# A transformer layer on one core: the first norm over four loads with a pivot, and first groups of one feature tile

## The chip, the cores and the metric

The kernel runs on one core of a Trainium2 chip. The metric is device microseconds (us) of one execution. A core has a matrix engine (TensorE, in the profile PE, with its weight loads as PEld), three engines for element-wise work (VectorE or DVE, ScalarE or ACT, GpSimd or POOL), and queues that issue DMA transfers, of which SyncE's (SP) brings nearly all data here. Each engine runs its own instructions strictly in the order in which they were written down, and waits on semaphores for what others make.

## The reference

One layer over 288 tokens (256 of a prompt, 8 sequences of 4), width 2048, all in float32, cut to what the change touches:

```python
mod = jax.nn.silu(c) @ w_ada + b_ada                      # 9 rows of c, 6 * 2048 columns
sh1, sc1, g1, sh2, sc2, g2 = jnp.split(mod[:, None, :], 6, axis=-1)
h = layer_norm(x) * (1 + sc1) + sh1
z = (h @ w_in).astype(f32)                                # 7176 columns
# ... two kinds of recurrent heads over z, output projection, two norms,
#     a gated convolutional FFN of width 5504, a last norm
```

`layer_norm` takes off the mean over the 2048 features and divides by the root of the variance plus 1e-5.

## The kernel before, in words

Features lie on partitions, tokens along the free axis: x is 16 tiles `xs[k]` of [128, 288]. TensorE multiplies weights as two exact parts, high and low, so a k-tile of 128 features times a column of 128 outputs takes three matmuls of 288 columns: high weights times the high and the low part of h, low weights times the high part. Weights stream in **granules** of up to 1024 columns (512 KB each): SP loads `raw`, ScalarE casts the high part (`whi`), VectorE subtracts to get the low part (`wlo`).

`start()` does the following, and the order in which it is written is the order on each engine.
- It loads x, then forms the mean: `colsum` adds up the features by a product with ones, `total` adds the four partial sums. It subtracts the mean from each tile, squares, adds up again, and takes `rx`, the inverse root, with one Newton step.
- The adaLN projection runs in **steps** (`ada_step`), each on 512 KB of `w_ada` (`araw`, four buffers, so a load waits until the step four before it has run). Steps form **units**: the shifts and scales of a few feature tiles. When the last step of a unit is done, `ada_finish` transposes its sums and writes `mod`, and `hidden(k)` makes h of each of its tiles on VectorE (times `rx`, times scale plus shift), with a cast on ScalarE (`split`) and a subtraction for the low part.
- The first 28 output columns of w_in are multiplied **group** by group: a group is some k-tiles (`KG`), for which its granules go through all 28 columns. The products of a column in a group stand in a PSUM bank until `partial` takes them into `z`: by a copy on ScalarE in the first group, by an add on VectorE in later ones. Banks alternate between tags `mm` (two buffers) and `sd` (five, shared with adaLN units and sums). Between granules some adaLN steps run, by a fixed rule.
- A group can begin when all its tiles of h exist.

Before, `KG` is (2, 2, 4, 4, 4), so the first two groups have 7 granules of 4 columns, 0.8 us of products a column, and units hold (2, 2, 2, 2, 4, 4) tiles. Eight steps run before the first product. `mixer()` follows with the last group, the other columns, the heads and the output projection, `tail()` with the rest. x lies in 16 buffers of the pool of [128, 288] tiles that everything shares.

Lines of the profile: L168 is every matmul, L155 tensor-tensor, L158 scalar-tensor-tensor, L162 tensor-scalar, L165 activation, L188 the cast of `split`, L228 the cast of weights, L389 the copy in `total`, L339 the transpose of a unit, L497 the copy of a column, L307 and L219 the loads of `w_ada` and weights, L436 of x.

Of the kernel before, what the change touches and what calls it, by code (L numbers as in the profile page):

```python
# [17 lines left out]
P = 128  # L18
# [30 lines left out]
KG = (2, 2, 4, 4, 4)  # L49
ADA_K = (2, 2, 2, 2, 4, 4)  # L50
# [74 lines left out]
def _ada_units():  # L125
    """The adaLN projection in units of 4 or 8 feature tiles (of 6 * 16)"""
    u, k = [], 0
    for n in ADA_K:
        u.append([16 * m + k + q for m in range(2) for q in range(n)])
        k += n  # L130
    return u + [[16 * m + 8 * z + q for q in range(8)] for m in range(2, 6) for z in range(2)]
# [6 lines left out]
class K:  # L138
    """One pass over the layer: features on partitions, the 288 tokens along the free axis.

    The weights stream through in granules of 1024 columns, each split into two exact parts of 12 bits;
    between granules the recurrences of the finished heads advance by a few steps.
    """
# [9 lines left out]
    # ---------------------------------------------------------------- small helpers  # L153
# [30 lines left out]
    def split(self, src, hi=None, lo=None):  # L184
        """src = hi + lo exactly, both of 12 significant bits."""
# [6 lines left out]
    # ---------------------------------------------------------------- weight stream  # L192
    def queue_weights(self):
        i, q = self.i, []
        for g, ks in enumerate(KG):
            if g == len(KG) - 1:
                q.append(i["w_gate"])
            q += [i[f"w_in_a{g}"][p] for p in range(NSPLIT * ks // GK)]
# [48 lines left out]
    def products(self, ps, hl, c0, xs, first, last, w=P):  # L247
        """ps += (hi + lo) of the weight tiles at columns c0... times xs, in three exact passes."""
# [15 lines left out]
    # ---------------------------------------------------------------- interleaving  # L264
    def tick(self):
        """advance the background work"""
# [4 lines left out]
    def slot(self):  # L271
        """Between two granules: advance the recurrences and the adaLN stream."""
# [10 lines left out]
    def later(self, *fs):  # L283
        """one of fs in each of the next slots"""
# [6 lines left out]
    def settle(self):  # L291
        """emit what is still to come of the background work"""
        while self.bg:
            self.tick()

    # ---------------------------------------------------------------- adaLN parameters
# [13 lines left out]
    def ada_step(self):  # L310
        """A k-tile or two of the columns of a unit of silu(c) @ w_ada, a quarter of the columns per column tile
        of the array: column tile q has the features 32 q ... 32 q + 31 of each of the unit's feature tiles."""
# [50 lines left out]
    # ---------------------------------------------------------------- statistics  # L363
    def rstd_of(self, v, pool=False):
        """v ** -0.5 with one Newton step; [128, 288]."""
# [15 lines left out]
    def colsum(self, ps, t, k, n):  # L381
        """partial sums over the features, in four column tiles of the array"""
# [3 lines left out]
    def total(self, ps):  # L386
        """32 times the sum of the partial sums, on every partition"""
# [6 lines left out]
    def log1pexp(self, src):  # L394
        """ln(1 + exp(-|src|))"""
# [6 lines left out]
    # ---------------------------------------------------------------- program  # L402
    def run(self):
# [21 lines left out]
        self.start()  # L425
# [3 lines left out]
    def start(self):  # L429
        """LN of x; then, as the adaLN parameters of each four k-tiles arrive, those k-tiles of h."""  # L430
# [3 lines left out]
        xs = self.xs = [self.t288() for _ in range(KT)]  # L434
        for k in range(KT):
            nc.sync.dma_start(xs[k], i["xt"][:, k, :])  # L436
        self.ada_load(NA)
        a, b = CC["cap"][0], PK["b_ada"][1]
        nc.sync.dma_start(self.cs[:, :a], i["cst"][:, :a])
        nc.sync.dma_start(self.pks[:, :b], i["pk"][:, :b])  # L440
# [8 lines left out]
        sm = self.ps(T)  # L449
        for k in range(KT):  # L450
# [1154 lines left out]
```

## Time and profile before

| | us |
|---|---|
| three runs | 1624.29, 1624.74, 1627.13 (median 1624.74) |
| profiled execution, span from first to last instruction | 1626.7 |
| TensorE busy | 1575.5 (97%) |
| VectorE busy | 1033.7 (64%) |
| ScalarE busy | 696.8 (43%) |
| GpSimd busy | 295.0 (18%) |
| chain that ended last | TensorE 87%, VectorE 8%, ScalarE 2%, DMA 1% |

The profiled execution has no other time than its span; this lies 2.0 us above the median of the runs. Busy times overlap, so they don't add up to the span. The chain that ended last is followed back from the last instruction, at each step to what released it; its shares say where the time is decided.

### The profile page before, as it was taken

What the parts mean: (1) busy time and instruction counts of PE and PEld (TensorE: products, weight loads), DVE (VectorE), ACT (ScalarE), POOL (GpSimd) and SP (SyncE); (2) the same over time, 40 slices, a digit from 0 to 9 for tenths busy, and PEclk for the clock granted to TensorE, in tenths of its full rate; (3) what the DMA queues carried; (4) which work ended last, traced back from release to release, by engine and by line L of the source; (5) the groups of instructions that cost most, each with busy time, mean ns of one, the idle gap of its engine ahead of it and who ended that gap; (6) DMA issues with size and microseconds to landing.
All of it is one profiled execution on the core that took longest, in us unless ns stands there. A gap on an engine that the chain in (4) does not pass through costs nothing.

```text
span 1626.7 us, 31719 instructions
## 1 busy us (share of the span) xinstructions
PE 1575.5 (97%) x12577; PEld 1445.1 (89%) x12577; DVE 1033.7 (64%) x2068; ACT 696.8 (43%) x1222; POOL 295.0 (18%) x450
## 2 busy tenths in 40 slices
PE   6999999999999999998999999999999999999995
PEld 3988889788888878886999999999999999999984
DVE  4566667877778778778865554455555455555445
ACT  3423235564655655435643433344443334334332
POOL 1000011444343343214411100011110001111012
PEclk9999999999999999999999999999999999999997
DMA  8988855767868777882545555555455554555441
GB/s 283 342 329 307 303 193 177 267 233 271 284 229 314 240 282 269 305 328 101 167 167 169 166 162 162 172 167 166 163 163 159 168 172 166 169 168 157 150 133 59
DMA packets 99268, 340.78 MB, mean 209 GB/s; under 512 B 11433, under 2 KB 18097, under 8 KB 98097
## 3 DMA queue, kind: packets, MB, share of 16 engines
q1 hardware_dynamic: 96624, 328.55, 59.8%
q0 software_dynamic: 2496, 10.22, 1.6%
q8 instruction: 99, 1.62, 0.4%
q14 instruction: 49, 0.39, 0.1%
HBM read 326.51 MB, written 12.21 MB: 208 GB/s over the span
## 4 chain that ended last, share of the span: by engine, by line
PE 87%; DVE 8%; ACT 2%; DMA 1%; issue 1%; SPq 0%; POOL 0%; ACTq 0%; DVEq 0%
PE mm L168 70%; PE sd L168 13%; PE ad L168 4%; DVE t L155 4%; DVE wlo L155 1%; DVE t L158 1%; ACT t L165 1%; DVE c L158 1%; ACT whi L228 1%; DVE t L162 1%; DMA araw<-w_ada 0%; DMA t<-xt 0%; DMA raw<-w_up_a 0%; PE sd L697 0%; PE sd L1066 0%
## 5 line engine op out<-in xcount | busy, mean ns | idle before, releaser
L168 PE MATMUL mm<-t,whi 128*128 128x288 f32 (+1 forms) x4624 | 940.4, 298 | 14.6 <-ACT whi L228 9.2
L168 PEld LDWEIGHTS mm<-t,whi 128*128 128x128 f32 (+1 forms) x4624 | 740.7, 188 | 39.2 <-issue 19.3
L168 PE MATMUL mm<-t,wlo 128*128 128x288 f32 x2312 | 682.6, 295 | 1.1 <-DVE wlo L155 1.1
L228 ACT CAST whi<-raw 128x1024 fp32r<-128x1024 f32 (+2 forms) x413 | 422.8, 1026 | 476.0 <-PE mm L168 242.2
L155 DVE TENSOR_TENSOR wlo<-raw,whi 128x1024 fp32r<-128x1024 f32 (+2 forms) x413 | 502.5, 1218 | 21.3 <-ACT whi L228 8.7
L168 PEld LDWEIGHTS mm<-t,wlo 128*128 128x128 f32 x2312 | 435.6, 188 | 1.7 <-DVE wlo L155 1.7
L168 PE MATMUL mm<-ff,whi 128*128 128x288 f32 x1376 | 276.8, 297 | 0.0
L168 PEld LDWEIGHTS mm<-ff,whi 128*128 128x128 f32 x1376 | 220.4, 188 | 6.2 <-issue 5.1
L168 PE MATMUL mm<-ff,wlo 128*128 128x288 f32 x688 | 203.1, 295 | 0.0
L165 ACT ACTIVATE t<-t 128x288 f32<-128x288 f32 (+4 forms) x328 | 125.7, 396 | 176.3 <-DVE t L155 117.6
L155 POOL TENSOR_TENSOR t<-t,t 128x288 f32<-128x288 f32 (+3 forms) x159 | 142.0, 903 | 294.6 <-ACT t L165 102.8
L158 DVE SCALAR_TENSOR_TENSOR t<-mm,mod,t 128x256 f32<-128x256 f32 x96 | 46.3, 483 | 155.7 <-PE mm L168 149.6
L168 PEld LDWEIGHTS mm<-ff,wlo 128*128 128x128 f32 x688 | 129.1, 188 | 0.0
L155 DVE TENSOR_TENSOR t<-t,t 128x288 f32<-128x288 f32 (+5 forms) x219 | 106.9, 508 | 34.1 <-ACT t L188 27.2
L1404 POOL COPY convo<-ext 128x2 f32<-128x2 f32 x43 | 7.9, 184 | 630.6 <-ACT ext L1398 630.6
L1399 DVE COPY ext<-mm 128x32 f32<-128x32 f32 x42 | 8.1, 192 | 141.9 <-ACT ext L1398 141.9
L168 PE MATMUL sd<-t,whi 128*128 128x288 f32 x464 | 95.9, 299 | 0.0
L168 PE MATMUL ad<-araw,csp 128*32 128x256 f32 (+1 forms) x1312 | 90.1, 368 | 5.8 <-DVE adsb L339 4.0
L168 PEld LDWEIGHTS sd<-t,whi 128*128 128x128 f32 x464 | 76.0, 192 | 0.0
L155 DVE TENSOR_TENSOR t<-t,mm 128x288 f32<-128x288 f32 x70 | 31.5, 451 | 65.5 <-PE mm L168 65.2
L155 DVE TENSOR_TENSOR t<-cv,mm 128x256 f32<-128x256 f32 x80 | 20.8, 301 | 78.3 <-PE mm L168 78.3
L168 PE MATMUL sd<-t,wlo 128*128 128x288 f32 x232 | 69.2, 298 | 0.0
(233 smaller groups left out, 1160.0 us busy)
## 6 DMA issues: line engine op xcount, KB each, us to landing
araw<-w_ada SPq DMA_DIRECT2D x180, 512.0 KB, 5.2
raw<-w_up_b SPq DMA_DIRECT2D x160, 512.0 KB, 3.6
raw<-w_in_a SPq DMA_DIRECT2D x56, 512.0 KB, 6.1
raw<-w_in_b SPq DMA_DIRECT2D x56, 512.0 KB, 5.3
raw<-w_down SPq DMA_DIRECT2D x48, 512.0 KB, 3.5
raw<-w_down SPq DMA_DIRECT2D x32, 384.0 KB, 3.1
raw<-w_out_a SPq DMA_DIRECT2D x16, 512.0 KB, 5.8
raw<-w_out_b SPq DMA_DIRECT2D x16, 512.0 KB, 6.0
```

The lines of the kernel that those rows point to most:

```text
L155: (eng or self.nc.vector).tensor_tensor(out=out, in0=a, in1=b, op=op)
L158: self.nc.vector.scalar_tensor_tensor(out=out, in0=a, scalar=s, in1=b, op0=op0, op1=op1)
L162: (eng or self.nc.vector).tensor_scalar(out=out, in0=a, scalar1=s1, scalar2=s2, op0=op0, **kw)
L165: self.nc.scalar.activation(out, a, f, **kw)
L168: self.nc.tensor.matmul(out, lhsT, rhs, start=start, stop=stop, **kw)
L228: self.nc.scalar.copy(hi[:, :w], raw[:, :w])
L1399: nc.vector.tensor_copy(se[:, :, 2:6], self.smp(pa))
L1404: nc.gpsimd.tensor_copy(co[:, j, 0:2], ext[:, TP:TP + 2])
```

## The change: what it does

x comes in four loads of four tiles into one tile `x` of a pool of its own (`xin`), which is closed after `start()`. The mean of the first four tiles is a **pivot**; it is taken off every tile as it lands (VectorE three of four, GpSimd one of four), ScalarE squares what is left, and two sums run side by side, of the deviations (`s1`) and of their squares (`s2`). The variance is the mean square less the square of the mean deviation `d`. `d` itself is taken off later: on GpSimd for tiles 4 to 15, and in `hidden` on VectorE for the first four.

`KG` becomes (1, 1, 2, 4, 4, 4), with granules of 7 columns of one tile, 4 columns of two tiles and 2 columns of four (`PER`); units hold (1, 1, 2, 4, 4, 4) tiles. Four steps run before the first product, and `ADA_DUE` says how many steps go into each group, spread over all its granules but the last. There is one granule more (57 for 56), and 28 more adds into `z`.

```diff
-KG = (2, 2, 4, 4, 4)
-ADA_K = (2, 2, 2, 2, 4, 4)
+KG = (1, 1, 2, 4, 4, 4)
+ADA_K = (1, 1, 2, 4, 4, 4)
+ADA_DUE = (4, 10, 16, 16, 24)
+PER = {1: 7, 2: 4, 4: 2}
...
-        xs = self.xs = [self.t288() for _ in range(KT)]
-        for k in range(KT):
-            nc.sync.dma_start(xs[k], i["xt"][:, k, :])
+        xt = xin.tile([P, KT, T], F32, name="x")
+        for k in range(0, KT, 4):
+            nc.sync.dma_start(xt[:, k:k + 4, :], i["xt"][:, k:k + 4, :])
+        xs = self.xs = [xt[:, k, :] for k in range(KT)]
         self.ada_load(NA)
         a, b = CC["cap"][0], PK["b_ada"][1]
+        nc.sync.dma_start(self.pks[:, :b], i["pk"][:, :b])
+        self.load_to(2)
         nc.sync.dma_start(self.cs[:, :a], i["cst"][:, :a])
-        nc.sync.dma_start(self.pks[:, :b], i["pk"][:, :b])
...
-        sm = self.ps(T)
-        for k in range(KT):
-            self.colsum(sm, xs[k], k, KT)
-        mu = self.t288()
-        self.tsc(mu, self.total(sm), 1.0 / (32 * D), None, ALU.mult)
-        self.ada_step()
-        self.ada_step()
-        sq = self.ps(T)
-        for k in range(KT):
-            self.tt(xs[k], xs[k], mu, ALU.subtract, eng=nc.gpsimd if k % 3 == 2 else None)
-            s = self.t288()
-            if k % 4 == 3:
-                self.tt(s, xs[k], xs[k], ALU.mult)
-            else:
+        pv = self.ps(T)
+        for k in range(4):
+            self.colsum(pv, xs[k], k, 4)
+        piv = self.t288()
+        nc.scalar.mul(piv, self.total(pv), 1.0 / (32 * 4 * P))
+        s1, s2 = self.ps(T), self.ps(T)
+        for c in range(0, KT, 4):
+            sq = []
+            for k in range(c, c + 4):
+                self.tt(xs[k], xs[k], piv, ALU.subtract, eng=nc.gpsimd if k % 4 == 2 else None)
+                s = self.t288()
                 self.act(s, xs[k], AF.Square)
-            self.colsum(sq, s, k, KT)
-            if k % 4 == 1:
-                self.ada_step()
-        var = self.t288()
-        self.tsc(var, self.total(sq), 1.0 / (32 * D), EPS, ALU.mult, ALU.add)
+                sq.append(s)
+            for k in range(c, c + 4):
+                self.colsum(s1, xs[k], k, KT)
+            for k in range(c, c + 4):
+                self.colsum(s2, sq[k - c], k, KT)
+        t1, t2 = self.total(s1), self.total(s2)
+        var, w = self.t288(), self.t288()
+        d = self.d = self.t288()
+        self.act(var, t2, AF.Identity, scale=1.0 / (32 * D), bias=self.eps)
+        self.tsc(d, t1, 1.0 / (32 * D), None, ALU.mult)
+        self.tt(w, d, d, ALU.mult)
+        self.tt(var, var, w, ALU.subtract)
         self.rx = self.rstd_of(var)
+        for k in range(4, KT):
+            self.tt(xs[k], xs[k], d, ALU.subtract, eng=nc.gpsimd)
...
-        self.load_to(2)
-        for _ in range(2):
-            self.tick()
+        for _ in range(4):
             self.ada_step()
...
-                for _ in range(2 if done < 13 or done % 3 == 0 else 1):
+                owed += ADA_DUE[g] / (NSPLIT // nj - 1) if p < NSPLIT // nj - 1 else 0
+                while owed > 0.5:
+                    owed -= 1
                     self.ada_step()
-                done += 1
...
     def hidden(self, k):
         x = self.xs[k]
         hf = self.t288()
+        if k < 4:
+            self.tt(x, x, self.d, ALU.subtract)
         self.tt(x, x, self.rx, ALU.mult)
```

The order on the engines moves at three places. On SP's queue behind the loads of x, before: all loads of `w_ada` that eight steps need and more (`araw`) stand ahead of the first two granules (`raw`).

```order
L307 DMA araw_118<-w_ada 128x1024
L439 DMA cs<-cst 128x168
L440 DMA pks<-pk 128x96
L307 DMA araw_162<-w_ada 128x1024
L307 DMA araw_181<-w_ada 128x1024
L307 DMA araw_207<-w_ada 128x1024
L307 DMA araw_233<-w_ada 128x1024
L307 DMA araw_259<-w_ada 128x1024
L219 DMA raw_318<-w_in_a 128x1024
L219 DMA raw_320<-w_in_a 128x1024
```

The same place now:

```order
L309 DMA araw_94<-w_ada 128x1024
L444 DMA pks<-pk 128x96
L221 DMA raw_97<-w_in_a 128x896
L221 DMA raw_99<-w_in_a 128x896
L446 DMA cs<-cst 128x168
L309 DMA araw_282<-w_ada 128x1024
L309 DMA araw_300<-w_ada 128x1024
L309 DMA araw_318<-w_ada 128x1024
L221 DMA raw_358<-w_in_a 128x896
```

The first two granules now stand behind four loads of `w_ada` and the small `pks`; the third stands behind three more.

On VectorE, where a unit of two tiles ends, before (`adsb` is the transposed unit, `t_886` and `t_891` its two tiles of h, `t_293` to `t_296` parts of z, `sd` and `mm` PSUM banks):

```order
L155 TENSOR_TENSOR t_293<-t_293,sd_833 128x288
L339 STREAM_TRANSPOSE adsb_875<-ad_668 128x128
L158 SCALAR_TENSOR_TENSOR mod<-adsb_875,pks 128x18 x2
L155 TENSOR_TENSOR t_84<-t_84,t_283 128x288
L162 TENSOR_SCALAR t_886<-t_84,mod 128x256
L155 TENSOR_TENSOR t_886<-t_84,mod 128x32
L155 TENSOR_TENSOR t_886<-t_886,mod 128x32
L155 TENSOR_TENSOR t_85<-t_85,t_283 128x288
L162 TENSOR_SCALAR t_891<-t_85,mod 128x256
L155 TENSOR_TENSOR t_891<-t_85,mod 128x32
L155 TENSOR_TENSOR t_891<-t_891,mod 128x32
L155 TENSOR_TENSOR t_294<-t_294,mm_867 128x288
```

Now, at the end of the second group, where the unit of two tiles ends (`t_213` is `d`, `t_218` the inverse root):

```order
L341 STREAM_TRANSPOSE adsb_816<-ad_653 128x128
L160 SCALAR_TENSOR_TENSOR mod<-adsb_816,pks 128x18 x2
L157 TENSOR_TENSOR wlo_831<-raw_614,whi_765 128x1024
L157 TENSOR_TENSOR t_257<-t_257,mm_799 128x288
L157 TENSOR_TENSOR x<-x,t_213 128x288
L157 TENSOR_TENSOR x<-x,t_218 128x288
L164 TENSOR_SCALAR t_842<-x,mod 128x256
```

The low part of a granule, an add and the subtraction of `d` now stand between the unit's transpose and its tiles. Some rows on, behind the second tile, come the low parts of h and only then the adds that free the banks of the group's last granule (columns `mm_837`, `sd_854`, `mm_867`, `sd_872`, `mm_877` and two more):

```order
L157 TENSOR_TENSOR t_859<-t_842,t_858 128x288
L157 TENSOR_TENSOR t_863<-t_848,t_862 128x288
L157 TENSOR_TENSOR t_258<-t_258,mm_837 128x288
L157 TENSOR_TENSOR t_259<-t_259,sd_854 128x288
L157 TENSOR_TENSOR t_260<-t_260,mm_867 128x288
```

On VectorE at the end of the third group, the last low part of the unit of four tiles and the add that frees the bank `mm_1227`, which the first column of the fourth group takes over:

```order
L157 TENSOR_TENSOR t_1271<-t_1245,t_1270 128x288
L157 TENSOR_TENSOR t_1275<-t_1250,t_1274 128x288
L157 TENSOR_TENSOR t_261<-t_261,mm_1227 128x288
L157 TENSOR_TENSOR t_262<-t_262,sd_1255 128x288
L157 TENSOR_TENSOR t_263<-t_263,mm_1279 128x288
```

What moved there: before, a unit ended two or three granules ahead of the group that reads its tiles; now one granule and at most two steps lie between.

More of the change, by code (lines that the diff above doesn't have):

```diff
@@ L197, in queue_weights @@
                 q.append(i["w_gate"])
-            q += [i[f"w_in_a{g}"][p] for p in range(NSPLIT * ks // GK)]
+            q += [i[f"w_in_a{g}"][p] for p in range(NSPLIT // PER[ks])]
         for n in range(56 - NSPLIT):
@@ L424, in run, with start @@
         self.ad_stop, self.ad_tag = AD0 - 4, "sd"
-        self.start()
+        with tc.tile_pool(name="xin", bufs=1) as xin:
+            self.start(xin)
         self.mixer()
         self.tail()
-    def start(self):
+    def start(self, xin):
         nc, i = self.nc, self.i
@@ L448, in start @@
         self.tt(self.csp[:, :, 0:9], ct, e, ALU.mult)
-        sm = self.ps(T)
-        for k in range(KT):
-            self.colsum(sm, xs[k], k, KT)
-        mu = self.t288()
-        self.tsc(mu, self.total(sm), 1.0 / (32 * D), None, ALU.mult)
-        self.ada_step()
-        self.ada_step()
-        sq = self.ps(T)
-        for k in range(KT):
-            self.tt(xs[k], xs[k], mu, ALU.subtract, eng=nc.gpsimd if k % 3 == 2 else None)
-            s = self.t288()
-            if k % 4 == 3:
-                self.tt(s, xs[k], xs[k], ALU.mult)
-            else:
-                self.act(s, xs[k], AF.Square)
-            self.colsum(sq, s, k, KT)
-            if k % 4 == 1:
-                self.ada_step()
-        var = self.t288()
-        self.tsc(var, self.total(sq), 1.0 / (32 * D), EPS, ALU.mult, ALU.add)
+        pv = self.ps(T)
[9 more added lines that the diff above has]
+                s = self.t288()
+                self.act(s, xs[k], AF.Square)
+                sq.append(s)
[10 more added lines that the diff above has]
+        self.tt(var, var, w, ALU.subtract)
         self.rx = self.rstd_of(var)
+        for k in range(4, KT):
+            self.tt(xs[k], xs[k], d, ALU.subtract, eng=nc.gpsimd)
         self.h = []
         self.z = [self.t288() for _ in range(NSPLIT)]
-        self.load_to(2)
-        for _ in range(2):
-            self.tick()
+        for _ in range(4):
             self.ada_step()
-        k0, done = 0, 0
+        k0, owed = 0, 0.0
         for g, ks in enumerate(KG[:-1]):
@@ L479, in start @@
                 self.tick()
-            nj = GK // ks
+            nj = PER[ks]
             for p in range(NSPLIT // nj):
@@ L1520, in prepare @@
     for n, ks in enumerate(KG):
-        nj = GK // ks
+        nj = PER[ks]
         arr[f"w_in_a{n}"] = np.ascontiguousarray(
```

## The prediction

> **What bounds the kernel now.** I read the windows by stage first, then the timeline of the first 40 us, then the places where TensorE stands idle. Windows: stretch, length, busy time and count of TensorE, weight load, VectorE (DVE), ScalarE (ACT), GpSimd (POOL), then granted clock, DMA share, GB/s.
>
> ```profile
> core 0: us, PE busy (x) PEld busy (x) DVE busy (x) ACT busy (x) POOL busy (x), PEclk, DMA share, GB/s
> 0.00:33.15 33.15, 19.16 (x196) 8.38 (x196) 15.15 (x35) 10.83 (x25) 6.64 (x15) 0.99 0.89 301
> 33.15:97.12 63.97, 63.21 (x736) 57.34 (x736) 39.00 (x82) 27.80 (x50) 0.00 (x0) 0.95 0.89 327
> 97.12:211.90 114.78, 114.78 (x977) 96.64 (x976) 68.82 (x130) 32.46 (x36) 0.00 (x0) 1.00 0.84 307
> ```
>
> From 33.15 us on TensorE is busy nearly all the time (63.21 of 63.97, then all of 114.78), and its work from there is fixed. So a gain must come from an earlier first product, and whatever idles TensorE later is paid in full, since a queue that is full to the end has no slack to give it back. What sets the first product is the chain through the norm (timeline: start, us, engine, line, operation, count):
>
> ```profile
> 3.85 7.63 PE L168 MATMUL sd<-t,ones 128*32 128x288 f32 x28 [3.85 <-DMA t<-xt]
> ...
> 11.66 1.30 PE L168 MATMUL sd<-t,ones 128*32 128x288 f32 x4 [0.18 <-DMA t<-xt]
> ...
> 14.73 2.41 DVE L155 TENSOR_TENSOR t<-t,t 128x288 f32<-128x288 f32 x3
> 14.78 4.95 POOL L155 TENSOR_TENSOR t<-t,t 128x288 f32<-128x288 f32 x5 [13.00 <-DVE t L162]
> ...
> 15.28 0.64 PE L168 MATMUL ad<-araw,csp 128*32 128x128 f32 x16 [1.07 <-DVE t L155]
> ...
> 20.83 0.82 DVE L155 TENSOR_TENSOR t<-t,t 128x288 f32<-128x288 f32 x2
> ...
> 24.77 0.40 ACT L389 COPY t<-sd 128x288 f32<-128x288 f32 x1 [1.21 <-PE sd L168]
> ...
> 26.50 0.92 ACT L165 ACTIVATE t<-t 128x288 f32<-128x288 f32 x2 [1.33 <-DVE t L162]
> ...
> 27.45 0.46 DVE L155 TENSOR_TENSOR t<-t,t 128x288 f32<-128x288 f32 x1 [0.98 <-ACT t L165]
> ...
> 28.81 0.31 DVE L339 STREAM_TRANSPOSE adsb<-ad 128x128 f32<-128x128 f32 x1
> ...
> 29.34 0.45 DVE L155 TENSOR_TENSOR t<-t,t 128x288 f32<-128x288 f32 x1
> ```
>
> ```profile
> 23.16 0.46 DVE L155 TENSOR_TENSOR t<-t 128x288 f32<-128x288 f32 x1
> ...
> 32.08 1.99 ACT L228 CAST whi<-raw 128x1024 fp32r<-128x1024 f32 x2
> ...
> 33.17 0.85 PE L168 MATMUL mm<-t,whi 128*128 128x288 f32 x2 [6.19 <-ACT whi L228]
> ...
> 34.44 0.61 PE L168 MATMUL mm<-t,wlo 128*128 128x288 f32 x1 [0.41 <-DVE wlo L155]
> ```
>
> x lands until 11.66, the mean is ready at 14.73, the deviations and squares end at 23.62 (23.16 + 0.46), the variance at 26.50, its root at 28.81, the first unit's shifts and scales at 29.34; the first product runs at 33.17, the first with low weights (all later ones follow without a gap) at 34.44. One VectorE subtraction takes 0.80 us (2.41 / 3) while GpSimd works, and 0.41 (0.82 / 2) without it; a GpSimd one takes 0.99.
>
> The windows around two places where TensorE stood idle, for the clock and the rate of the loads:
>
> ```profile
> 26.90:33.10 6.20, 0.08 (x4) 0.00 (x0) 4.84 (x16) 2.27 (x6) 0.00 (x0) 0.93 1.01 409
> 33.10:38.90 5.80, 5.31 (x20) 4.96 (x21) 3.59 (x3) 3.04 (x6) 0.00 (x0) 0.50 0.68 271
> ...
> 310.10:312.20 2.10, 0.02 (x4) 0.00 (x0) 2.07 (x3) 0.53 (x2) 0.73 (x2) 0.97 0.95 372
> 312.20:318.60 6.40, 6.15 (x30) 5.35 (x31) 5.78 (x21) 3.99 (x13) 2.28 (x4) 0.50 0.96 350
> ```
>
> **Start, part by part.** The first load landed at 3.85; the first of four carries 0.44 MB more, 1.1 us at the 409 GB/s of these windows, so about 5.0. Pivot: before took 3.07 from the last landing to the mean, so 8.1. Subtractions: GpSimd's four take 4.0 us, in which VectorE does five of its twelve; the other seven take 2.9: 15.0. ScalarE's squares run beside it, the last ends at 15.45. From there to the variance before took 2.9 (23.62 to 26.50), and the new form subtracts d squared on VectorE as well. But as soon as d is known, at about 17.5, GpSimd starts on `x - d` for k = 4...15: 12 x 0.99 = 12 us, until 29.5, beside the whole rest of the chain. So 0.80 for that subtraction (19.2), 0.95 for Ln and Exp, 3 x 0.80 for the Newton step (22.5), 0.53 for transpose and `mod` (28.81 to 29.34), then for the first tile 0.80 (x - d), 0.80 and some 0.65 for the rest (25.3), a cast of 0.43 and the high weights 0.95 (half of 1.99, at 7/8 width a little less): first product 26.7. The low weights are a VectorE subtraction too; beside GpSimd one took 1.83:
>
> ```profile
> 284.19 0.83 POOL L155 TENSOR_TENSOR t<-t,t 128x288 f32<-128x288 f32 x1 [13.47 <-ACT t L165]
> 284.26 1.83 DVE L155 TENSOR_TENSOR wlo<-raw,whi 128x1024 fp32r<-128x1024 f32 x1
> ```
>
> 7/8 of that is 1.6: 28.3 instead of 34.44, **-6.1 us**. Ends: six chain subtractions at 0.41 and low weights at 1.1 give -9; if each waits a whole GpSimd instruction, 0.6 more each, -2.5. I take the middle, since 0.80 was measured on these same subtractions. The Trainium skill ("SBUF — State Buffer", Terms) says that VectorE and GpSimd hold one port pair as an exclusive lock and the loser blocks for the full instruction; by that the sum below would be 3.6 higher. The trace agrees only in part: 0.80 is less than 0.41 + 0.99. The loads aren't late: 5.5 MB (x, four steps, two granules) at 409 GB/s is 13.5 us. `pks` moves ahead of weights on SP and `cs` behind them; `cs` is first needed in the mixer. GpSimd's twelve subtractions now stand ahead of memsets and a mask cast that are read in the mixer alone, after 212.
>
> **adaLN steps.** Before ran 8 steps while TensorE was idle anyway, after runs 4. Two steps take 1.01 us:
>
> ```profile
> 52.77 0.81 PEld L168 LDWEIGHTS sd<-araw,csp 128*32 128x32 f32 x32 [0.17 <-issue]
> 52.77 1.08 PE L168 MATMUL sd<-araw,csp 128*32 128x128 f32 x32
> ...
> 53.78 0.53 PE L168 MATMUL mm<-t,whi 128*128 128x288 f32 x2
> ```
>
> so the 4 now on TensorE's time cost 4 x 0.505 = 2.0. A step of the first two units has 16 matmuls of 64 columns in place of 8 of 128: twice the weight loads, 32 x 25 ns (0.81 / 32) = 0.81 where 0.505 stood; four of these eight are on the path: +1.2. Together **+3.2** (2.0 if the loads hide, 4.3 at 1.08 a step).
>
> **The ends of groups.** Before, a unit's last step stood two or three granules ahead of the first product that reads its tiles; now one granule and at most two steps. What VectorE must do in between stands in the trace, for a unit of four tiles, whose last step ended where the next product began, at 138.39:
>
> ```profile
> 138.39 0.53 PE L168 MATMUL mm<-t,whi 128*128 128x288 f32 x2
> ...
> 138.53 0.45 DVE L339 STREAM_TRANSPOSE adsb<-ad 128x256 f32<-128x256 f32 x1
> ...
> 139.23 0.45 DVE L155 TENSOR_TENSOR t<-t,t 128x288 f32<-128x288 f32 x1
> ...
> 140.38 0.45 DVE L155 TENSOR_TENSOR t<-t,t 128x288 f32<-128x288 f32 x1
> ...
> 143.81 0.45 DVE L155 TENSOR_TENSOR t<-t,mm 128x288 f32<-128x288 f32 x1
> 144.18 1.22 DVE L155 TENSOR_TENSOR wlo<-raw,whi 128x1024 fp32r<-128x1024 f32 x1
> 145.32 1.56 DVE L155 TENSOR_TENSOR t<-t,t 128x288 fp32r<-128x288 f32 x4
> 146.79 0.45 DVE L155 TENSOR_TENSOR t<-t,sd 128x288 f32<-128x288 f32 x1
> ```
>
> 0.14 to the transpose, 0.70 to the first tile, 1.15 for each tile, 0.37 for an add from PSUM, 1.14 for low weights, 1.47 for the four low parts, 0.45 for the add that frees the next bank: no idle TensorE there, since two more granules covered it. Now the ends one by one, a column of three matmuls being 0.40 us (six take 0.80, chain of work: start, us, engine, count):
>
> ```profile
> 59.25 0.80 PE sd L168 x6
> ```
>
> - First to second group (one tile): 0.14 + 0.5 + 1.64 + 0.43 + 0.45 = 3.2 against 7 columns, 2.8; ScalarE's PSUM copies queue behind the cast. **+1.2** (0.4 to 2).
> - Second to third (two tiles, each with x - d, +0.49): 0.14 + 0.53 + 1.14 + 0.37 + 2 x 1.64 + 0.96 = 6.4, then the add of `mm_837`, 6.9. Only two banks carry the tag `mm`, so TensorE does two steps (1.0) and four columns (1.6), stands from 2.6 to 6.9, then ends its three columns. Without waits 3.8; so **+4.4**.
> - Third to fourth (four tiles): 0.14 + 0.70 + 1.14 + 0.37 + 4.58 + 1.47 + 0.45 = 8.85 until `mm_1227` is added and its bank free; TensorE is there after two steps and four columns of 0.80, at 4.2: **+4.65** and idle throughout.
> - Later ends have two or more granules (11 us against 8.9): nothing.
>
> **The clock after a wait.** Where TensorE stood, it came back at half the granted clock (windows above): 6.2 us idle, then 5.8 at 0.50; 2.1 us idle, then 6.4 at 0.50. The start has this before and after alike. Two new idle stretches of 4.3 and 4.65 lie between those, so each costs about half of 6 us: **+6.0** (0 to 6.4; the gap of 1.07 at 15.28 cost no clock, since the first stage shows 0.99). The Trainium skill ("TensorE: Matmul & The Clock Gate", Part 1) says that an idle window of 3.4 us halves the clock and 3.4 us of work restores it: 1.7 each, a sum 2.6 lower. The trace agrees on the half, but 2.1 us was enough here and the return took 6.
>
> **Loads.** In the third group a granule brings 0.52 MB and 16/7 steps as much each, 1.72 MB in 3.2 + 1.15 us: 396 GB/s. The windows show up to 409, and where both ran,
>
> ```profile
> 41.20:97.10 55.90, 55.58 (x678) 50.43 (x676) 34.24 (x79) 23.37 (x43) 0.00 (x0) 1.00 0.95 346
> ```
>
> 346. At 346 seven granules would take 4.4 us more; but the waits at both ends let the queue fill its buffers. **+1** (0 to 5), of which some is the second group's, whose steps 13 and 14 come hard on their loads. The 28 more adds from PSUM (10 us of VectorE at 0.37) lie beside products, except as counted.
>
> **Sum.** -6.1 + 3.2 + 1.2 + 4.4 + 4.65 + 6.0 + 1.0 = +14.35 us on the profiled span of 1626.7, so 1641.1. The median of the runs, 1624.74, lies 2.0 below that span; I forecast **1639**, slower by 0.9%.
>
> **Rivals.** (a) The waits come, the clock doesn't fall or comes back sooner: +8.4, 1633. For it: idle gaps of about 1 us left the clock at full; against it 2.1 us did not. (b) Loads pace the third group as well: +4 on top, 1643 to 1645; for it the 346. (c) The port lock takes whole instructions: the start gains 2.5, 1643. (d) Faster: the chain beside GpSimd runs at 0.41, so the start gains 9, and VectorE has the tiles ready before TensorE asks, as at 138.5 to 147: -9 + 3.2 + 1.2 + 1 = -3.6, 1621. It decides if both ends and the clock together cost under 1.5 us; against it, 6.9 and 8.85 us of VectorE rows stand against 2.6 and 4.2 of TensorE's. (e) About even: the start gains 9 and only one end waits, without a fall of the clock, +1, 1626: the change then moves the idle time and doesn't shorten it.
>
> **How the numbers follow.** Forecast 0.47, (a) 0.17, (b) 0.08, (c) 0.05, (d) 0.13, (e) 0.10. 0.2% (3.2 us) is about what a measurement of this kernel tells from no change. Faster is (d), 0.13; same (e), 0.10; slower 0.77. The forecast with (a) to (c) spans 1630 to 1648; down to 1624 the range takes in (e) and leaves out (d) and a tail above.
>
> **What will show it.** First product near 26.7, low-weight one near 28.3; VectorE tensor ops near 0.8 beside twelve GpSimd ones from 17.5; two TensorE waits of over 4 us released by VectorE, near 65 and 102 us, clock 0.50 behind each; TensorE full from there to 212 + 14. Wrong if those waits are under 2 us, the first product comes before 25, or loads release TensorE in the third group for more than 3 us.

## The result, and the profile after

The changed kernel takes **1645.6 us** (median of 1644.55, 1645.48, 1645.74 and 1648.88) against 1625.9 for the kernel before (the three times given ahead and a fourth of 1628.05): ratio **1.0121** (95% interval 1.0108 to 1.0135), 1.2% slower. The forecast was 1639 with a range of 1624 to 1648. The profiled execution has a span of 1642.5 us, 15.8 more than before's 1626.7; in the changed kernel an execution's time is 2.0 above its span.

The span falls into three stretches, up to the first product, from there to the first product of the gates (the one of `w_gate`, where the mixer begins), and the rest. The windows of the changed kernel (columns as in the prediction), and of before for the second and third:

```profile
0.00:30.60 30.60, 14.03 (x206) 6.50 (x206) 17.20 (x30) 12.68 (x31) 15.79 (x24) 0.89 0.78 297
30.61:233.47 202.86, 188.28 (x1728) 158.81 (x1729) 122.51 (x248) 60.91 (x87) 0.56 (x2) 0.95 0.78 284
233.47:1642.50 1409.03, 1372.51 (x10655) 1278.56 (x10653) 909.44 (x1822) 625.25 (x1113) 289.36 (x435) 0.99 0.58 194
```

```profile
33.17:211.91 178.74, 178.00 (x1712) 153.97 (x1712) 107.80 (x211) 60.24 (x85) 0.00 (x0) 0.98 0.86 314
211.91:1626.70 1414.79, 1378.35 (x10673) 1282.80 (x10669) 910.77 (x1822) 625.70 (x1113) 288.34 (x435) 0.99 0.58 194
```

The first product runs at 30.6 in place of 33.2: -2.6 us. From it to the gates 202.9 us pass in place of 178.7: **+24.1**, of which 13.8 are idle time of TensorE (14.6 for 0.7). The rest of the program is 5.8 shorter. Together 15.8.

What TensorE waited for most between 30.6 and 234 us (the view of waits: total, times, longest), and the four longest of these waits in its timeline:

```profile
PE mm L170 <- DVE t L157: 6.9, 3, 3.5
PE ad L170 <- DMA araw<-w_ada: 4.8, 4, 2.3
...
PE sd L170 <- DMA araw<-w_ada: 0.8, 2, 0.6
```

```profile
59.28 0.65 PE L170 MATMUL ad<-araw,csp 128*32 128x128 f32 x16 [1.32 <-DMA araw<-w_ada]
62.26 1.08 PE L170 MATMUL ad<-araw,csp 128*32 128x128 f32 x16 [2.33 <-DMA araw<-w_ada]
...
75.81 0.85 PE L170 MATMUL mm<-t,whi 128*128 128x288 f32 x2 [3.53 <-DVE t L157]
...
117.16 0.51 PE L170 MATMUL mm<-t,whi 128*128 128x288 f32 x2 [3.05 <-DVE t L157]
```

VectorE's work for new tiles costs 6.9 us, the loads of step weights 5.6 (4.8 + 0.8); low weights and one copy of a column make 1.6 (0.8 each). The busy time of the stretch grew by 10.3 as well. For that the windows around the changes of the clock:

```profile
61.00:61.30 0.30, 0.00 (x0) 0.00 (x0) 0.00 (x0) 0.27 (x1) 0.00 (x0) 0.68 1.05 423
67.80:68.10 0.30, 0.30 (x3) 0.30 (x3) 0.10 (x1) 0.00 (x0) 0.00 (x0) 0.77 0.04 14
74.60:74.90 0.30, 0.00 (x0) 0.00 (x0) 0.20 (x1) 0.30 (x2) 0.00 (x0) 0.77 0.90 369
81.40:81.70 0.30, 0.30 (x4) 0.30 (x3) 0.30 (x1) 0.00 (x0) 0.00 (x0) 0.68 0.00 0
...
117.20:120.00 2.80, 2.80 (x21) 2.80 (x22) 2.80 (x6) 0.97 (x1) 0.00 (x0) 1.00 0.43 110
```

The clock column changes inside the first four rows: full speed ends near 61.1 and near 74.8, and comes back near 67.9 and 81.6. So there are two spells of 6.8 us at half clock, the first begun in the load waits, the second in the wait of 3.5; the third long wait (3.05, to 117.16) left the clock at 1.00. TensorE worked for 5.7 us of the first spell (from 62.26) and 5.8 of the second (from 75.81) and lost half of that, 5.7 together. Six more adaLN steps lie in this stretch than before (70 for 64), 3.0 us at 0.5 each. The half clock of the start also reaches further, over 6.3 us of the first products (to 37.2) where it was 5.4 before (to 39.0): 0.5. 1.1 us of the 10.3 are not assigned.

The start, with VectorE's chain, GpSimd's work beside it and the first products:

```profile
19.83 0.84 DVE L157 TENSOR_TENSOR t<-t,t 128x288 f32<-128x288 f32 x1
...
25.00 2.01 DVE L157 TENSOR_TENSOR x<-x,t 128x288 f32<-128x288 f32 x2
...
27.73 0.77 DVE L157 TENSOR_TENSOR t<-x,mod 128x32 f32<-128x32 f32 x1
28.54 0.71 DVE L157 TENSOR_TENSOR t<-t,mod 128x32 f32<-128x32 f32 x1
```

```profile
19.34 10.62 POOL L157 TENSOR_TENSOR x<-x,t 128x288 f32<-128x288 f32 x12 [6.17 <-PE sd L170]
```

```profile
30.61 0.85 PE L170 MATMUL mm<-t,whi 128*128 128x288 f32 x2 [9.43 <-ACT whi L230]
31.74 0.61 PE L170 MATMUL mm<-t,wlo 128*128 128x288 f32 x1 [0.28 <-DVE wlo L157]
```

From the variance to the first tile VectorE's operations are stretched, those of 32 columns (0.77, 0.71) no less than those of 288 (0.84, and 1.0 each of the two of 2.01); how long they take alone, the first experiment shows.

### The profile page after: what moved, and what is told of

The parts are those of the page before. It is cut to its first block, busy times and chain, and to the rows that moved or that the text cites. A ratio compares the mean times of both kernels' runs of the same rounds, so it can differ in the third digit from the quotient of the medians.

```text
span 1642.5 us, 31800 instructions
## 1 busy us (share of the span) xinstructions
PE 1574.8 (96%) x12587; PEld 1443.9 (88%) x12587; DVE 1049.2 (64%) x2099; ACT 698.9 (43%) x1230; POOL 305.7 (19%) x461
## 4 chain that ended last, share of the span: by engine, by line
PE 83%; DVE 11%; ACT 2%; DMA 2%; issue 1%; SPq 0%; POOL 0%; ACTq 0%
PE mm L170 67%; PE sd L170 12%; DVE t L157 4%; PE ad L170 3%; DVE wlo L157 2%; DVE t L160 2%; DMA araw<-w_ada 1%; ACT t L167 1%; DVE t L164 1%; DVE c L160 1%; ACT whi L230 1%; DVE x L157 0%; DMA pks<-pk 0%; DMA x<-xt 0%; DMA raw<-w_up_a 0%
## 5 line engine op out<-in xcount | busy, mean ns | idle before, releaser
L170 PE MATMUL mm<-t,wlo 128*128 128x288 f32 (+1 forms) x2316 | 685.1, 296 | 2.2 <-DVE wlo L157 2.2
L170 PEld LDWEIGHTS mm<-t,wlo 128*128 128x128 f32 (+1 forms) x2316 | 437.5, 189 | 3.5 <-DVE wlo L157 3.5
L167 ACT ACTIVATE t<-t 128x288 f32<-128x288 f32 (+4 forms) x316 | 120.8, 395 | 171.6 <-DVE t L157 117.6
L157 POOL TENSOR_TENSOR t<-t,t 128x288 f32<-128x288 f32 (+3 forms) x154 | 137.8, 904 | 281.3 <-ACT t L167 99.6
L157 DVE TENSOR_TENSOR t<-t,t 128x288 f32<-128x288 f32 (+4 forms) x193 | 94.4, 509 | 29.7 <-ACT t L190 22.9
L170 PE MATMUL ad<-araw,csp 128*32 128x256 f32 (+2 forms) x1312 | 86.2, 363 | 7.7 <-DMA araw<-w_ada 4.8
L157 DVE TENSOR_TENSOR t<-t,mm 128x288 f32<-128x288 f32 x86 | 38.7, 451 | 74.7 <-PE mm L170 74.4
```

The lines of the kernel that those rows point to most:

```text
L157: (eng or self.nc.vector).tensor_tensor(out=out, in0=a, in1=b, op=op)
L167: self.nc.scalar.activation(out, a, f, **kw)
L170: self.nc.tensor.matmul(out, lhsT, rhs, start=start, stop=stop, **kw)
```

## Experiments

Times of the first product and of the gates' first one are from each kernel's timeline; "rest" is the span behind the gates. The kernel before had medians of 1626.4 to 1626.5 beside these runs.

| kernel | median us | ratio to before (95%) | first product | gates | rest |
|---|---|---|---|---|---|
| before | 1625.9 | 1 | 33.2 | 211.9 | 1414.8 |
| changed | 1645.6 | 1.0121 (1.0108 to 1.0135) | 30.6 | 233.5 | 1409.0 |
| e1_hold | 1642.8 | 1.0097 (1.0082 to 1.0112) | 26.0 | 229.7 | 1410.7 |
| e2_norm | 1627.2 | 1.0008 (0.9999 to 1.0018) | 34.7 | 213.1 | 1411.9 |
| e3_groups | 1648.6 | 1.0133 (1.0117 to 1.0150) | 32.2 | 234.0 | 1412.8 |
| e4_araw8 | 1639.0 | 1.0078 (1.0063 to 1.0093) | 30.6 | 226.8 | 1410.2 |
| e5_warm | 1637.3 | 1.0063 (1.0048 to 1.0079) | 30.4 | 221.6 | 1415.4 |
| e6_pre | 1636.4 | 1.0062 (1.0047 to 1.0076) | 30.6 | 221.6 | 1415.6 |
| e7_comb | 1622.9 | 0.9974 (0.9964 to 0.9984) | 29.8 | 207.5 | 1411.2 |
| e8_comb2 | 1623.2 | 0.9973 (0.9962 to 0.9983) | 27.5 | 208.8 | 1412.6 |
| e9_warm_consts | 1632.5 | 1.0037 (1.0023 to 1.0051) | 30.6 | 222.5 | 1407.8 |
| e10_all | 1630.7 | 1.0023 (1.0014 to 1.0033) | 26.0 | 219.5 | 1410.9 |

**Hold GpSimd back (e1_hold).** From the changed kernel:

```diff
-        for k in range(4, KT):
-            self.tt(xs[k], xs[k], d, ALU.subtract, eng=nc.gpsimd)
...
+            if g == 0:      # once h[0] exists, ahead of the first group
+                nc.gpsimd.tensor_copy(self.t288()[:, :1], self.h[0][1][:, :1].bitcast(F32))
+                for k in range(4, KT):
+                    self.tt(xs[k], xs[k], d, ALU.subtract, eng=nc.gpsimd)
```

> The changed kernel, with GpSimd's twelve `x - d` held until the first tile's low part is ready, so that no GpSimd operation lies beside the chain from the variance to the first product. Theory (the port shared by the two engines slows every VectorE operation of that chain): 32-column operations go from 0.77 to 0.2 us, 288-column ones from 0.8-1.0 to 0.46, together 4.5 us, so the first product comes at 26 to 27 in place of 30.6, and the total falls by about 4 (1641 to 1642). Rival (the chain is long for another reason, ScalarE's casts or the steps): first product at 30 or later, total within 1 us. Third possibility: the start gains 4 and the loads of the second group, which already made TensorE wait 3.6 us, give it back there: total down by less than 2.

The same rows of VectorE, with the low weights behind them, and two of TensorE:

```profile
19.66 0.46 DVE L157 TENSOR_TENSOR t<-t,t 128x288 f32<-128x288 f32 x1
...
22.91 0.94 DVE L157 TENSOR_TENSOR x<-x,t 128x288 f32<-128x288 f32 x2
...
24.22 0.18 DVE L157 TENSOR_TENSOR t<-x,mod 128x32 f32<-128x32 f32 x1
24.44 0.19 DVE L157 TENSOR_TENSOR t<-t,mod 128x32 f32<-128x32 f32 x1
...
25.97 4.80 DVE L157 TENSOR_TENSOR wlo<-raw,whi 128x896 fp32r<-128x896 f32 x3 [0.38 <-ACT whi L230]
```

```profile
25.99 0.85 PE L170 MATMUL mm<-t,whi 128*128 128x288 f32 x2 [4.97 <-ACT whi L230]
...
57.04 0.65 PE L170 MATMUL ad<-araw,csp 128*32 128x128 f32 x16 [1.93 <-DMA araw<-w_ada]
```

The same operations take 0.46 for 0.84, 0.18 for 0.77, 0.19 for 0.71; added up, all that VectorE does in this chain falls from 8.8 to 4.3 us. The first product comes 4.6 earlier, as the theory had it to 0.1. The price moved to the low weights, now beside GpSimd (1.6 each, 4.80 / 3). Of the 4.6, 3.8 are left at the gates, 2.8 in the median. The load waits of the second group are there again (1.93 here, 1.50 just ahead of it), and TensorE, earlier at the third end, waits 4.1 there, with 6.8 us at half clock from 109.6 that the changed kernel doesn't have.

**The two halves of the change (e2_norm, e3_groups).** The new norm with the old groups, and the old norm with the new groups:

```diff
 e2_norm, from the changed kernel
-KG = (1, 1, 2, 4, 4, 4)
-ADA_K = (1, 1, 2, 4, 4, 4)
...
+KG = (2, 2, 4, 4, 4)
+ADA_K = (2, 2, 2, 2, 4, 4)
...
-        for _ in range(4):
+        for _ in range(8):
             self.ada_step()
...
+                for _ in range(2 if done < 13 or done % 3 == 0 else 1):
...
 e3_groups, from the kernel before
-KG = (2, 2, 4, 4, 4)
-ADA_K = (2, 2, 2, 2, 4, 4)
+KG = (1, 1, 2, 4, 4, 4)
+ADA_K = (1, 1, 2, 4, 4, 4)
+ADA_DUE = (4, 10, 16, 16, 24)
+PER = {1: 7, 2: 4, 4: 2}
...
-            if k % 4 == 1:
+            if k in (5, 13):
                 self.ada_step()
...
```

> The new norm alone: four loads of x, sums about a pivot, the moved loads, but groups and units of two tiles as before and the 8 steps ahead of the first product. Theory (the slowdown lies in the smaller groups, and the new norm gains little because GpSimd slows the chain): first product between 32 and 34, no TensorE wait over 1 us in the groups, total within 3 us of the kernel before. Rival (the moved loads or GpSimd's work cause the later waits): total over 1632.

> The smaller first groups and units alone, with the old norm (four of the steps run in the norm, none between norm and first product). Theory: the same waits at the ends of the second and third group (3 to 4 us each), load waits of 3 us or more in the second group and two stretches at half clock, so +17 to +20 over the kernel before, 1642 to 1646, since the start hardly differs (first product 31 to 33). Rival (the grouping alone costs only the waits, no clock and no loads): +8, 1634.

TensorE's rows of the norm alone, then of the groups alone:

```profile
25.30 0.67 PE L169 MATMUL ad<-araw,csp 128*32 128x128 f32 x16 [1.52 <-DMA araw<-w_ada]
...
34.69 0.85 PE L169 MATMUL mm<-t,whi 128*128 128x288 f32 x2 [5.42 <-ACT whi L229]
```

```profile
74.26 0.85 PE L170 MATMUL mm<-t,whi 128*128 128x288 f32 x2 [2.55 <-DVE t L157]
...
116.31 0.50 PE L170 MATMUL mm<-t,whi 128*128 128x288 f32 x2 [3.26 <-DVE t L157]
```

The norm alone is worth nothing (+0.7 us, within the noise), the groups alone cost **22.1**. In the norm alone the last four of the eight steps wait for their loads until 28 us, since there are four buffers; the first product is then 1.5 later than before and 0.7 later than the latest I expected, with no wait in the groups but 0.2 us for a load. The groups alone show the waits of the changed kernel at the same ends (2.55 and 3.26) and load waits of 5.5 us; half clock comes behind the loads of the second group, the second end and the third (3.4, 6.8 and 3.4 us). They cost 2.6 more than the top of what was expected. So the slowdown lies in the groups. Joined to them, the norm is worth 2.9 us (1645.6 for 1648.6; 2.4 when each is compared with before's times beside it), but 3.8 of the 4.2 us between the two profiles lie behind the gates, where the groups alone had more half clock (20.5 us for 6.8; see below).

**Eight buffers for the steps (e4_araw8).**

```diff
...
-            if not ahead and s >= (self.ad_n if s < AD0 else max(self.ad_n, AD0 + NPRE)) + NA:
+            if not ahead and s >= (self.ad_n if s < AD0 else max(self.ad_n, AD0 + NPRE)) + (8 if s < 64 else NA):
...
+            elif s < 64 and s % 2:
+                raw = self.xin.tile([P, 1024], F32, tag="araw2", name=self.nm("araw2"), bufs=4)
             else:
                 raw = self.wp.tile([P, 1024], F32, tag="araw", name=self.nm("araw"), bufs=NA)
...
-        self.ada_load(s + NA)
+        self.ada_load(s + (8 if s < 56 else NA))
...
```

> The changed kernel with eight buffers for the weights of the adaLN steps in place of four until step 64. In the changed kernel the loads stand still at 17 to 21 and 30 to 36 us because the buffers are full. Theory (the buffers, not the rate, make TensorE wait for steps): the load waits of the second and third group (5.6 us together) mostly go, and with them the half clock from 62 to 68: 4 to 8 us less than the changed kernel, 1637 to 1642. Rival (the rate of about 350 GB/s is the limit): the waits move later and the total changes by less than 2 us.

TensorE's waits from 30 to 228 (one of 0.8 left out), and the two spells at half clock:

```profile
PE mm L170 <- ACT whi L230: 9.4, 1, 9.4
PE mm L170 <- DVE t L157: 8.6, 3, 4.7
PE mm L170 <- DVE wlo L157: 0.8, 2, 0.5
...
```

```profile
66.50:73.30 6.80, 4.72 (x20) 4.73 (x21) 5.82 (x14) 2.29 (x3) 0.00 (x0) 0.50 0.98 390
107.40:114.30 6.90, 6.24 (x28) 5.97 (x32) 4.44 (x9) 1.43 (x3) 0.00 (x0) 0.51 0.41 144
```

No load wait remains, and behind the second group's loads the clock doesn't fall: -6.6 us. The loads had the rate and lacked buffers. VectorE's waits grew from 6.9 to 8.6, since TensorE now arrives earlier at the third end (4.7 for 3.05); with 4.7 idle the clock fell there too, so that there are two spells as before. From the first product to the gates, 4.1 of the 6.7 us gained are idle time.

**Keep TensorE at work in the waits (e5_warm).**

```diff
+                if (g, p) == (3, 0):
+                    self.warm(32)
                 for j in range(nj):
+                    if (g, p, j) == (1, 3, 4):
+                        self.warm(24)
...
+    def warm(self, n):
+        ps = self.ps(T)
+        for _ in range(n):
+            self.mm(ps, self.onesr, self.h[0][0], True, True)
```

> The eight-buffer kernel with useless products where TensorE stood idle there: 24 ahead of the product that waited 3.5 us at 68.6, 32 ahead of the one that waited 4.7 us at 108.1 (0.13 us each at full clock, 3.2 and 4.3 us), into a bank that nothing reads. The releases by VectorE stay where they are. Theory (the idle time drops the clock, and the half clock behind it costs work): the clock stays at 1.00 from 66 to 73 and from 107 to 114, where the two spells of 6.8 us slowed 4.7 and 6.2 us of work to half, so 5 us less than the eight-buffer kernel, 1634. Rival (the clock falls for another reason, the rate of work before, say): same time within 1 us, or up to 2 slower where the useless products run late.

Windows of both places and of one in the mixer, then VectorE and TensorE there:

```profile
65.60:72.40 6.80, 6.37 (x45) 5.76 (x44) 6.20 (x16) 1.48 (x2) 0.00 (x0) 1.00 1.01 404
102.20:109.00 6.80, 6.40 (x51) 6.03 (x53) 6.69 (x17) 2.90 (x5) 0.00 (x0) 1.00 0.70 249
232.00:240.50 8.50, 7.32 (x29) 7.00 (x30) 3.92 (x7) 1.82 (x3) 0.00 (x0) 0.50 0.25 78
```

```profile
226.92 0.17 DVE L157 TENSOR_TENSOR lbm<-pks 128x8 f32<-128x8 f32 x1 [6.24 <-DMA pks<-pk]
...
230.40 0.40 PE L170 MATMUL mm<-t,wlo 128*128 128x288 f32 x1 [2.05 <-DVE wlo L157]
```

The clock stays at 1.00 at both ends and the gates come 5.2 earlier (221.6 for 226.8), as expected: half clock costs what it was priced at. The median falls by 1.8 only. The next thing in line stands in the last rows: VectorE waits 6.2 us for the load of `pks`, which starts with the mixer, low weights queue behind that, TensorE waits for them, and the clock is at half for 10.2 us from 231.9. The rest is 5.2 longer.

**Load the mixer's constants earlier (e9_warm_consts)**, from e5_warm:

```diff
+                if (g, p) == (len(KG) - 2, 2):
+                    nc.sync.dma_start(self.cs[:, a:], i["cst"][:, a:])
+                    nc.sync.dma_start(self.pks[:, b:], i["pk"][:, b:])
                 hl = self.granule()
...
-            nc.sync.dma_start(self.cs[:, a:], i["cst"][:, a:])
-            nc.sync.dma_start(self.pks[:, b:], i["pk"][:, b:])
```

> The kernel with the useless products, with the mixer's constants loaded in the last group of the first stage. There the products of the gates came 5.2 us earlier than with eight buffers alone (221.6 against 226.8), yet the span stayed at 1637.0: VectorE waited 6.2 us for `pks`, TensorE 2.0 for low weights queued behind it, and the clock was half from 232 to 240. Theory (the load of the constants, which starts with the mixer and doesn't come earlier, took the gain back): no VectorE wait for `pks`, clock at 1.00 through 230 to 245, 4 to 5 us less, 1632 to 1633. Rival (the gates' own chain sets it, or the clock falls by its windows all the same): within 1.5 us, 1636 to 1638.

The window behind the gates:

```profile
222.46:245.00 22.54, 20.31 (x151) 19.67 (x150) 14.33 (x28) 7.25 (x10) 3.40 (x6) 1.00 0.53 175
```

The clock is at 1.00 there, the wait for `pks` is gone and the time falls by 4.8 to 1632.5: the gain had been taken back by that load. From e4_araw8 to here, work that computes nothing and an earlier load are worth 6.5 us.

**Shorten VectorE's work at the ends (e6_pre)**, from e4_araw8:

```diff
+            if g == 0:
+                nc.gpsimd.tensor_copy(self.t288()[:, :1], self.h[0][1][:, :1].bitcast(F32))
+                for k in range(2, KT):
+                    if k < 4:
+                        self.tt(xs[k], xs[k], d, ALU.subtract, eng=nc.gpsimd)
+                    self.tt(xs[k], xs[k], self.rx, ALU.mult, eng=nc.gpsimd)
...
-        if k < 4:
+        if k < 2:
             self.tt(x, x, self.d, ALU.subtract)
-        self.tt(x, x, self.rx, ALU.mult)
+            self.tt(x, x, self.rx, ALU.mult)
```

> The eight-buffer kernel with VectorE's work at the group ends shortened: GpSimd subtracts d from tiles 2 and 3 and multiplies tiles 2 to 15 by the root ahead of time, beside the first group, so that VectorE has 0.95 us less for each of tiles 2 and 3 and 0.49 less for each later tile when their shifts and scales come. Theory (VectorE's queue of the new tiles' work sets the waits): the wait of 3.5 us at the third group's begin falls to about 1.6, that of 4.7 at the fourth's to about 2.7, and one or both spells of half clock may go: 4 us less with both spells kept, up to 9 less without them. Rival (the bank, the step or ScalarE's cast sets those waits): unchanged within 1 us. GpSimd's 16 operations, of about 1 us each, slow the low weights of the first group, at most 0.8 us each, beside products that take 2.8.

TensorE at the three ends:

```profile
49.76 0.53 PE L170 MATMUL mm<-t,whi 128*128 128x288 f32 x2 [1.94 <-ACT t L515]
...
69.80 0.53 PE L170 MATMUL mm<-t,whi 128*128 128x288 f32 x2 [1.56 <-DVE t L157]
...
105.68 0.82 PE L170 MATMUL mm<-t,whi 128*128 128x288 f32 x2 [2.71 <-DVE t L157]
```

3.53 became 1.56 and 4.7 became 2.71, as computed from the VectorE rows that were taken away (2 x 0.95 and 4 x 0.49): VectorE's queue sets these waits. Behind the second end the clock no longer falls, behind the third half of the spell is left (105.0 to 108.5). GpSimd's 16 operations cost 1.2 at the first end (1.94 for 0.8), and there the clock now falls for 3.4 us. The gates come 5.2 earlier, and the mixer's load takes that back as in e5_warm (10.2 us at half clock from 231).

**A version that beats both (e7_comb, e8_comb2).** The new norm with groups and units of two tiles, e1's hold, e4's buffers, and four of the eight steps among the sums:

```diff
 e7_comb, from e2_norm with e1_hold and e4_araw8
+            for _ in range(2 if c == 12 else 0):
+                self.ada_step()
             for k in range(c, c + 4):
                 self.colsum(s2, sq[k - c], k, KT)
+            for _ in range(2 if c == 8 else 0):
+                self.ada_step()
...
-        for _ in range(8):
+        for _ in range(4):
             self.ada_step()
 e8_comb2, from e7_comb, and the constants as in e9_warm_consts
         self.rx = self.rstd_of(var)
+        self.high_to(2)
```

> A combination: the new norm, but groups and units of two tiles as before, GpSimd's twelve subtractions held until the first tile is ready, eight buffers for the steps, and four of the first eight steps put among the sums. Theory (the start can gain when nothing lies beside the chain, and the larger groups bring no waits): first product at 28 in place of 33.2, no TensorE wait over 1 us before the gates, total 5 us below the kernel before, 1621. Rival (the loads, at 354 GB/s from 48 to 100 us, already run at what the chain needs, so that an earlier start turns into load waits): gain under 2 us.

> The combination again, with the cast of the first weights put ahead of the first tile's on ScalarE, where it stands at 28.7 behind the cast of the second tile, and the mixer's constants (the rest of `pks` and `cs`) loaded in the last group of the first stage in place of the mixer's begin. Theory: first product at 28.8 in place of 29.8, and VectorE no longer waits for `pks` behind the gates: 1 to 3 us less than the combination, 1620 to 1622. Rival (VectorE's low weights set the start, and the wait for `pks` lies beside TensorE's work): within 1 us of it.

First products of e7_comb with its waits from 26 to 205, then of e8_comb2:

```profile
29.80 0.85 PE L169 MATMUL mm<-t,whi 128*128 128x288 f32 x2 [5.42 <-ACT whi L229]
31.08 0.61 PE L169 MATMUL mm<-t,wlo 128*128 128x288 f32 x1 [0.43 <-DVE wlo L156]
```

```profile
PE mm L169 <- ACT whi L229: 5.4, 1, 5.4
PE mm L169 <- DVE wlo L156: 0.4, 1, 0.4
```

```profile
27.53 0.61 PE L169 MATMUL mm<-t,whi 128*128 128x288 f32 x1 [2.84 <-ACT t L189]
...
31.39 0.61 PE L169 MATMUL mm<-t,wlo 128*128 128x288 f32 x1 [1.71 <-DVE wlo L156]
```

e7_comb takes **1622.9 us, ratio 0.9974** (0.9964 to 0.9984), faster than both kernels, with a first product 1.8 later than I expected and no wait of note from there to the gates, which come 4.4 earlier than before. e8_comb2 changes nothing: its first product with high weights is 2.3 earlier, the first one with low weights 0.3 later (31.39 for 31.08), since those are VectorE's and come behind both tiles. With the old groups VectorE's wait for `pks` (4.4 us in e7_comb) held up no product.

**All repairs on the new groups (e10_all).** e6_pre with both GpSimd parts held until the first tile is ready, and the constants early.

> The changed grouping with all that was found mended at once: GpSimd's work held until the first tile is ready, eight buffers for the steps, x - d and the product with the root done ahead of time on GpSimd for tiles 2 to 15, the constants loaded early. Theory (the times add): 4 for the start, 5 for the constants from the 1636 of the kernel with the work done ahead, so 1627, even with the kernel before and about 4 behind the combination with groups of two tiles: the waits at the group ends of 1 to 3 us and the steps on TensorE's path remain. Rival (the one-tile start wins once nothing stands in its way): 1621 or less. Other rival (GpSimd's 28 operations now slow VectorE in the first two groups): 1630 or more.

TensorE at the first end, and GpSimd:

```profile
46.22 0.53 PE L170 MATMUL mm<-t,whi 128*128 128x288 f32 x2 [2.38 <-ACT t L515]
```

```profile
25.84 29.11 POOL L157 TENSOR_TENSOR x<-x,t 128x288 f32<-128x288 f32 x28
```

1630.7: the pessimistic rival. The 28 GpSimd operations last until 55 us and stretch the second tile's work, so the first end waits 2.4 and the clock falls there for 3.4 us; at the third end, behind a wait of 2.7, it falls for 6.8. The groups of one tile stay 0.23% behind the kernel before and 7.8 us behind e7_comb, though their first product comes 3.8 earlier than e7_comb's.

## Why the prediction was right, and where its terms were off

The direction, the place and the mechanism held: the waits at the group ends and the clock behind them outweigh the earlier start. The sum on the span was +14.35 and came as +15.8. That it is off by 1.5 only is luck: the start was off by +3.5, the loads by +4.6, the ends by -2.4 and what lies behind the gates by -5.8, and these nearly cancel.

- **Start, -6.1, came as -2.6** (-2.7 at the product of low weights, for which the term was worked out). This term was mis-sized, to its lower bound of 2.5, and rival (c) was nearer. I priced each chain operation at the 0.80 measured on 288-column subtractions; but nearly each waits for GpSimd, 0.3 to 0.6 us whatever its size. The rule of the Trainium skill that the prediction set aside as half true ("SBUF — State Buffer", Terms: the port pair is held for the full instruction and the loser blocks) describes the 32-column rows (0.18 to 0.77) better than my price; e1_hold shows that GpSimd's work is the cause. The first product missed 26.7 by 3.9 us, and 1.5 of these were lost by the variance, before the twelve operations mattered: x was 0.6 later (5.62), and beside GpSimd VectorE's subtractions of the pivot came 0.97 us apart in place of 0.80 (the squares that wait for them start at 9.64, 10.62, 11.59, 12.55 and 13.52), so that ScalarE's squares ended at 17.29 for 15.45.
- **adaLN steps, +3.2.** Steps of 64 columns are not dearer: in the changed kernel four took 1.99 us, 0.50 each, their weight loads 14 ns each (1.83 / 128) for the 25 that I took. So +1.2 was nothing. In the stretch six steps came on top, not four; the two others leave the mixer.
- **Ends.** First +1.2: 0.9 (0.77 for a copy of a column, and short ones). Second +4.4: 3.9 (0.37 + 3.53), at the fifth of the seven columns, as the prediction had it. Third +4.65: 3.05, because the loads had held TensorE up just before (1.00 at 110); without load waits, in e4_araw8, 4.7.
- **Clock, +6.0: 5.7**, two spells of 6.8, but the first behind the loads of the second group instead of the third end. e5_warm and e9_warm_consts confirm that price.
- **Loads, +1, came as 5.6**, just beyond the bound of 5. I took the rate as the limit and overlooked that four buffers let the loads stand still while TensorE waits. The steps 13 and 14 that I named are where it struck (1.32 and 2.33). The line "wrong if loads release TensorE in the third group for more than 3 us" was drawn in the wrong group.
- **Behind the gates, 0: -5.8.** 1 us is the two steps fewer. Where before stood 2.32 us behind a unit's transpose and then worked 6.6 us at half clock (3.3 lost), the changed kernel waits 0.67 and keeps its clock:

```profile
312.45 1.08 PE L168 MATMUL ad<-araw,csp 128*32 128x256 f32 x8 [2.32 <-DVE adsb L339]
```

```profile
326.92 0.64 PE L170 MATMUL ad<-araw,csp 128*32 128x256 f32 x8 [0.67 <-DVE adsb L341]
```

  The wait goes with the units: 2.3 us in the profiles of before, e2_norm, e7_comb and e8_comb2, which have the old ones, 0.7 in all others. The half clock behind it doesn't: e7_comb kept its clock at 1.00 there. Nor do the spells further on, 10.2 us in before (from 749 and 769), 6.8 in the changed kernel, and 20.5 in e3_groups, which has the same groups and a rest of 1412.8 for 1409.0. So the 1.6 us of the wait are the change's, and how much half clock is saved beside it is luck.
- **Span to median.** I took 2.0 off, as if the profiled execution of before were typical. Executions of before lie 1.8 above their spans, so that one took about 1628.5, 2.6 above the median of 1625.9, and those of the changed kernel lie 2.0 above theirs. Of the 6.6 us between 1639 and 1645.6, 4 come from this conversion, 1.5 from the sum and 1.1 from the profiled execution being the fastest of its four.

The forecast's own branch happened, with both waits and two spells of half clock, but the signs named for it came in part: the waits were 3.5 and 3.05 us in place of over 4, they ended at 75.8 and 117.2, only the first brought half clock, the first product came at 30.6 for 26.7, and "TensorE full from there to 212 + 14" failed (the gates came at 233.5).

## What to carry to other kernels

Before cutting a pipeline's first stage finer, add up what must run between a stage's last input and the next stage's first product, on each engine: the finer cut leaves less cover for it, and every wait may bring a spell at half clock. Keep GpSimd's work away from a serial chain on VectorE, even if that work is needed soon; here 12 operations that nobody waited for yet held the first product back by 4.6 us. Where loads must catch up after a wait, ask whether they have buffers to run ahead in, before blaming the rate. After each gain look for the next fixed arrival (here `pks`) that may take it back.

## What the hardware showed that I had not expected

- **The clock changes on a grid.** In the changed kernel at 61.1, 67.9, 74.8 and 81.6: 6.8 us apart each. The Trainium skill ("TensorE: Matmul & The Clock Gate", Part 1) says that a free-running window of 3.413 us decides; two of these are 6.83, and the trace agrees. In all twelve profiles every spell from 20 to 340 us lasts 3.4, 6.8, 10.2 or 13.7 us, a whole number of windows. Where a wait falls in the grid matters: waits of 1.94, 2.55 and 3.5 us were followed by half clock (e6_pre, e3_groups, the changed kernel), one of 3.05 was not (the changed kernel). An idle window need not be empty, though; in the window that ends at 61.1, where the clock fell, TensorE was busy for 0.9 us:

```profile
57.70:61.10 3.40, 0.91 (x28) 0.38 (x16) 0.72 (x2) 0.07 (x1) 0.00 (x0) 1.00 1.02 396
```

- **Useless work pays.** 56 products that nobody reads, 7.5 us of TensorE's time at 0.13 each, brought the gates 5.2 us forward.
- **The stretch beside GpSimd doesn't shrink with the operation.** Beside GpSimd's operations of 0.89 us (10.62 / 12), VectorE's of 0.18 and 0.19 us became 0.77 and 0.71, its 0.46 became 0.84 and 0.74; GpSimd's own took 0.99 in the start before.
